# One more split of an inner product in five P7 stages of a soft-routing kernel, with VectorE's queue, the P7 weight sums and the start of P3 rearranged

## The chip, the cores and the metric

One core of a Trainium2 chip runs the kernel. Its time is device microseconds of one execution, and a figure for a kernel is the median of several runs. TensorE multiplies matrices, VectorE and ScalarE read its results out of PSUM (eight banks, each 512 fp32 columns on 128 partitions), GpSimd and SyncE issue DMAs here (ScalarE issues some too).

## The reference

```python
probs = softmax(router_logits)                  # (16, 512, 8)
for e in range(8):
    output += probs[:, :, e:e+1] * matmul(x, expert_weights[e])
# x (16, 512, 512), expert_weights (8, 512, 2048), output (16, 512, 2048), all float32
```

With the batch flattened there are 8192 rows. The sum over the experts is one product: the operand of a row is its x, times the probability of each of the 8 experts, side by side (8 x 512 long), and the weights of the experts stand one under the other.

## The kernel before, in words

**Outer products.** Rows come in 32 blocks of 256; a row pair q is the blocks 2q and 2q+1. The row pair, the two halves of the experts and the two halves of the output's columns (1024 each) make a 2 x 2 by 2 x 2 block product, which is done in seven products P1 to P7 instead of eight (the scheme of Strassen and Winograd) on sums and differences of operands and of weights. In the names of the code r is the number of the outer product (`product(r, q)`, `lefts[r, q]`, `right[r]`).

**Inner products.** Each outer product of a row pair is split in the same manner again. It becomes seven inner products (`STEPS`: 1, 5, 6, 2, 7, 3, 4 in time), each of 8 matrix multiplications of 128 x 128 by 128 x 512. "Step p" is one inner product p, and about 1.73 us of TensorE. Step 6 needs the operand difference `s2` (tile `d`) and accumulates onto the bank of step 1; steps 3 and 7 need the difference `i` (tile `z`), and steps 5, 6, 7 and 4 need weight differences (weight sums, tiles `w`, 128 x 4096), which are made once for each outer product.

**A third split.** In most stages inner products 1 and 5 of the two row pairs are split once more ("by thirds", `by_thirds`): the two row pairs stand as the two rows of a 2 x 2 product, and seven quarter-products take the place of eight. I call them quarters r, again in the order 1, 5, 6, 2, 7, 3, 4; each is 4 multiplications of 128 x 256. Such a split stage has 56 narrow multiplications in place of 32 wide ones. P2's stages of the beginning split inner product 2 (`by_twos`, class `Twos`) as well.

**Stages.** A stage is one or two outer products run together, step by step in turn. By number: 0 to 6 P1; 7 to 14 P2 (14 is called `last2`); 15 (`k5`) two P5; 16 a single P6; 17 to 30 a P6 of one row pair and a P5 of the next; 31 (`k6`) a single P6; 32 (`k7`) to 47 alternate, the even ones P7 and the odd ones P4 of the same two row pairs; 48 (`k3`) a single P3; 49 to 55 two P3 each; 56 a single P3. Inner products 1 and 5 are split in P4's stages from 35 on, and in P3's from 49 to 55. P7's stages are not split: 112 multiplications of 512 columns each.

**The order of the work.** TensorE's, VectorE's and ScalarE's programs are each one list, in the order in which the Python code emits them. For VectorE a planner decides. Work that is not tied to a step (operands, differences, weight sums) is wrapped by `later(cost, make)` into a `Task` and put in a queue. After each step, `slack` moves a clock of TensorE by the step's 1.73 us (0.44 for a quarter) and takes tasks from the queue while VectorE's own clock, which adds up costs, is behind:

```python
def slack(slot=SLOT, lag=LAG):
    clock["dve"] = max(clock["dve"], clock["pe"])
    clock["pe"] += slot
    while queue and clock["dve"] < clock["pe"] - lag:
        queue.popleft().run()
```

Then the step's own reading out of PSUM (the "eviction") is emitted by `post`: VectorE adds a bank to a base in SBUF (`ps<-ps,h`, `h<-ps,h`, `h<-pt,h`), or ScalarE copies it. A task that a step needs and that is not yet done is taken at once (`need`, `flush`). `at(stage, slot, make)` is a hook: `make` runs before step number `slot` of that stage. Hooks fetch weights and bases, put weight sums in the queue, and begin operands of later stages.

**Places of interest.** In stage 14 the hooks at slots 2, 4, 6 and 8 fetch four weight blocks of 1 MB, called `t2` (tile `w` from `wd`, on ScalarE's DMA queue), and slot 9 queues the weight sums 5 and 6 of P6 out of them, each one VectorE operation of 128 x 4096. In stage 14 every step has two evictions in turn, one for each row pair. P7's weight sums 6 and 7 are queued in stages 30 and 31, and 4 in stage 32. P3's weights are loaded into the places of P7's and P4's in stages 46 and 47 (`turnover_in_place(3, ...)`), and its sums 7 and 5 are queued at slot 3 of stage 47, 6 at slot 10, 4 at slot 3 of stage 48. The first P3 is of row pair 5. The first halves of the operands of row pairs 5, 8 and 10 for P3 (`EARLY`) are made during stages 20 and 24, stored, and loaded again in stage 47.

Of the kernel before, what the change touches and what calls it, by code (L numbers as in the profile page):

```python
# [31 lines left out]
def kernel(  # L32
# [41 lines left out]
    def x_tile():  # L74
        return xpool.tile([P, C, HQ], f16, name="xs", tag="x")

# [93 lines left out]
    def inner_sums(b, t7=None):  # L170

        w = {1: b[0, 0], 2: b[1, 0], 3: b[1, 1], 7: t7 or b[0, 1]}

        def step(p, x, y):
            if p not in w:
                w[p] = new_w()
            tt(w[p], x, y, SUB)
        return w, {5: lambda: step(5, b[0, 1], b[0, 0]), 6: lambda: step(6, b[1, 1], w[5]),
                   4: lambda: step(4, b[1, 0], w[6]), 7: lambda: step(7, b[1, 1], b[0, 1])}
# [178 lines left out]
    LAG = 0.3  # L358
# [89 lines left out]
    class Left:  # L448
# [35 lines left out]
        def queue_s2(self):  # L484
            def make():
                self.s2 = spool.tile([P, K8, HP], f16, name="d", tag="d")
                tt(self.s2, self.t[0][:, :, ds(HP, HP)], self.t[0][:, :, ds(0, HP)], SUB)
            self.task["s2"] = later(0.69, make)
# [51 lines left out]
    class HalfLoadedLeft(Left):  # L540


        def __init__(self, xb, pb, kept, source):
            super().__init__(xb, pb, kept=kept)
            self.source = source

        def load(self):
            self.t[0] = new_z()
            sp(self.t[0], self.source)

        def queue_make(self, k):
            if k == 0:
                self.task[0] = None
            else:
                super().queue_make(k)
# [14 lines left out]
    class Thirds:  # L570
# [17 lines left out]
        def queue(self):  # L588
            self.a.queue_make(0)
            self.b.queue_make(0)  # L590
            for p in (5, 6, 3, 7):
# [3 lines left out]
            for left in (self.a, self.b):  # L595
                left.queue_make(1)

        def op(self, p, part):
            need(self.task[7])
            a, b = self.a.t[0], self.b.t[0]  # L600
            z = {1: a[:, 0:C], 2: a[:, C:K8], 4: b[:, C:K8]}.get(p)
            return (self.s[p] if z is None else z)[:, :, ds(part * HP, HP)]

    class Right:
# [9 lines left out]
        def queue_sum(self, sums, p, first=False):  # L614
            def make():
                flush(self.task.get({6: 5, 7: 5, 4: 6}.get(p)))
                sums[p]()
            self.task[p] = later(2.29, make, first)
# [32 lines left out]
    class Product:  # L651
# [7 lines left out]
        def step(self, p):  # L659
            b = "q" if p in (5, 3) else "b" if p == 2 else "x"  # L660
            if p in (1, 5):
                self.banks[b] = (bank if p == 1 else bank2)()
# [100 lines left out]
    def left_of(r, q, fresh=True):  # L763
# [22 lines left out]
        if r == 3 and q in EARLY:  # L786
            pa = PBlock(a, P2)
            return HalfLoadedLeft(xblock(a), pa, ZHalf(q, z_places[q]), operand3[q]), [xblock(a), pa]
# [47 lines left out]
    EARLY = {5: (5, 3), 8: (8, 3), 10: (10, 9)}  # L836
    operand3 = {q: dram.tile([P, K8, HQ], f16, name=f"operand3_{q}") for q in EARLY}
    z_room = []

    def z_place(i):  # L840
        def place():
            if i != 2:
                z_room.append(new_w().rearrange("p k (two t) -> p (k two) t", two=2))
            return z_room[-1][:, ds(i // 2 * K8, K8), :]
        return place
    z_places = {q: z_place(i) for i, q in enumerate((5, 8, 10))}
# [93 lines left out]
    def by_twos(stage):  # L940
# [37 lines left out]
        def full(i, p):  # L978
            some[i].step(p)
            slack()  # L980
            some[i].post(p)
# [10 lines left out]

    def queue_lefts(stage):
        if stage in thirds:
            if not thirds[stage].task:
                thirds[stage].queue()
        elif stage < len(stages):
            for p in stages[stage]:
                queue_left(p.left)

    def run(stage):
# [5 lines left out]
        n = by_thirds(stage) if stage in thirds else 0  # L1007
        if stage in twos:
            n = by_twos(stage)
        for i in range(n // 2, len(some[0].steps)):  # L1010
            for p in some:
                for make in hooks.get((stage, n), ()):
                    make()
                p.step(p.steps[i])
                slack()
# [64 lines left out]
    def queue_halves(q, k):  # L1080
        for i in range(2):
            lefts[7, q + i].queue_make(k)
        if k == 0:
            for i in range(2):
                lefts[7, q + i].queue_s2()
    for n, q in enumerate(ORDER_7[1:], 1):
# [7 lines left out]
        for slot, k in ((5, 0), (11, 1)):  # L1094
            at(stage - 1, slot, lambda q=q, k=k: queue_halves(q, k))
# [208 lines left out]
    def turnover_in_place(r, raw, loads, sums):  # L1304
# [15 lines left out]
        for p, where in sums:  # L1320
            def go(p=p):
# [3 lines left out]
                      ((7, (k3 - 1, 3)), (5, (k3 - 1, 3)), (6, (k3 - 1, 10)), (4, (k3, 3))))  # L1325
# [14 lines left out]
    for stage, slot, q, k in ((k3 - 1, 2, 5, 0), (k3 - 1, 6, 5, 1), (k3 - 1, 7, 8, 0), (k3 - 1, 9, 10, 0),  # L1340
                              (k3 - 1, 10, 8, 1), (k3 - 1, 12, 10, 1)):
        left = lefts[3, q]
        at(stage, slot, left.load if k == 0 else left.kept.begin)
    at(k3, 0, load_z(0))
    early_p = {}

    def early_begin(q):
        early_p[q] = PBlock(2 * q, P2, h_tile([P, 2, HQ], f16))
        sp(early_p[q].t, p_dram[2 * q, ds(P2, 2), :].partition_broadcast(P))

    def early_make(q):
        of = lefts[6, q]
        flush(of.task[0])
        u = new_u()
        times(u, 0, of.xb, early_p[q])
        tt(u, u, of.t[0], SUB)
        sp(operand3[q], u)
    for q, (stage, slot) in EARLY.items():
        at(*slots_after(k5 + stage - 1, slot, 7), lambda q=q: early_begin(q))
        at(k5 + stage, slot, lambda q=q: later(2.45, lambda: early_make(q), True))  # L1360
# [14 lines left out]
    third_at(k3 - 1, 6, third3, 3, 5)  # L1375
# [24 lines left out]
    for p in (1, 5):  # L1400
        at(k7 + 1, 6, lambda p=p: third_sum(p, 7))

# [101 lines left out]
```

## Time and profile before

| | |
|---|---|
| median of 3 runs | 1354.31 us (1354.19 to 1354.35) |
| profiled execution, its own time | 1354.04 us |
| its span in the profile | 1352.3 us |
| TensorE (PE) busy | 1345.7 us, 7062 multiplications |
| weight loads (PEld) | 687.9 us, beside the multiplications |
| VectorE (DVE) busy | 1153.5 us, 1446 instructions |
| ScalarE (ACT) busy | 274.7 us |
| GpSimd (POOL) busy | 404.5 us |
| DMA | 346.12 MB, mean 256 GB/s |

The profile is one execution. Its own time is 1.74 us longer than its span, which lasts from the first to the last instruction that is shown. In its rows L133 is the line of all multiplications (`mm`), L110 that of all VectorE's additions, subtractions and products (`tt`); the tile names tell them apart: `ps` and `pt` are PSUM banks (`bank` and `bank2`), `z`, `u`, `xs` and `d` operands, `w` weights, `h` results and bases. A row of the timeline has start, duration, engine, line, operation with tiles, shape and count, and in brackets the idle time ahead of it with what ended it. A row of the stretches (`A:B`) has the length of the stretch and then, in order, busy time (and instructions) of TensorE, its weight loads, VectorE, ScalarE and GpSimd, then TensorE's clock, the DMA share and GB/s.

### The profile page before, as it was taken

How to read it: one execution, taken by the hardware profiler on the slowest of the kernel's cores; microseconds unless marked ns; L12 is line 12 of the kernel's file. 1: busy time of each engine (PE TensorE's matmuls, PEld its weight loads, DVE VectorE, ACT ScalarE, POOL GpSimd, SP SyncE). 2: the span in 40 equal slices, each digit the busy share in tenths (PEclk: the TensorE clock that was granted, in tenths of full speed). 3: DMA queues.
4: the chain of work that ended last, by engine and by line, in shares of the span. 5: the costliest groups of instructions: out<-in, count | busy, mean ns of one | idle time of the engine just before them, and what ended most of it. 6: DMA issues, size and time to landing. Idle time of an engine off the chain costs nothing.

```text
span 1352.3 us, 19284 instructions
## 1 busy us (share of the span) xinstructions
PE 1345.7 (100%) x7062; PEld 687.9 (51%) x7062; DVE 1153.5 (85%) x1446; ACT 274.7 (20%) x573; POOL 404.5 (30%) x619
## 2 busy tenths in 40 slices
PE   9999999999999999999999999999999999999998
PEld 4566655565544444444444444554555455556564
DVE  7878898888889889798887899888988988988886
ACT  3233423232211111111111100110111011224331
POOL 3223323333223332323312113424333221232342
PEclk9999999999999999999999999999999999999999
DMA  9999979999899999999988897999999989999997
GB/s 187 245 221 237 266 243 237 301 301 269 230 322 302 318 282 297 290 315 264 349 265 270 299 328 158 241 263 207 232 249 225 218 223 333 250 252 234 221 167 127
DMA packets 185391, 346.12 MB, mean 256 GB/s; under 512 B 52176, under 2 KB 81488, under 8 KB 181200
## 3 DMA queue, kind: packets, MB, share of 16 engines
q0 software_dynamic: 84960, 176.72, 57.5%
q1 hardware_dynamic: 97024, 146.02, 35.5%
q10 hardware_dynamic: 3312, 22.15, 4.5%
q8 instruction: 55, 0.90, 0.3%
q14 instruction: 40, 0.33, 0.1%
HBM read 203.59 MB, written 173.74 MB: 279 GB/s over the span
## 4 chain that ended last, share of the span: by engine, by line
PE 83%; issue 10%; POOL 3%; DMA 2%; DVE 1%; POOLq 0%; ACT 0%; DVEq 0%
PE ps L133 65%; PE pt L133 18%; POOL out_dram L124 2%; DMA w<-wd 1%; DMA wd<-w 1%; DVE h L110 1%; DMA out_dram<-h 1%; POOL wd L124 0%; DMA w<-in_x_dram 0%; DVE z L110 0%; POOL w L124 0%; POOL xs L124 0%; DVE w L110 0%; DVE ps L110 0%; POOLq L124 0%
## 5 line engine op out<-in xcount | busy, mean ns | idle before, releaser
L133 PE MATMUL ps<-w,z 128*128 128x512 f16 (+1 forms) x3784 | 818.3, 372 | 0.3 <-DVE z L110 0.3
L133 PEld LDWEIGHTS <-z 128*128 128x128 f16 x5256 | 514.1, 98 | 546.5 <-DVE z L110 0.8
L124 POOL DMA_DIRECT2D out_dram<-h x380 | 249.2, 663 | 729.7 <-ACT h L704 321.8
L133 PE MATMUL pt<-w,z 128*128 128x512 f16 (+1 forms) x1444 | 286.3, 343 | 0.0
L110 DVE TENSOR_TENSOR h<-ps,h 128x512 f32<-128x512 f32 x298 | 202.3, 687 | 81.5 <-PE ps L133 68.2
L110 DVE TENSOR_TENSOR z<-xT,pT 128x2048 f16<-128x2048 f16 x189 | 228.2, 1217 | 0.8 <-DMA xT<-xs 0.8
L133 PE MATMUL ps<-w,d 128*128 128x512 f16 x880 | 199.9, 379 | 0.6 <-DVE ps L110 0.6
L691 ACT COPY h<-ps 128x512 f32<-128x512 f32 x102 | 59.8, 586 | 393.9 <-PE ps L133 382.9
L133 PEld LDWEIGHTS <-d 128*128 128x128 f16 x880 | 86.1, 98 | 98.4 <-issue 1.2
L110 DVE TENSOR_TENSOR z<-z,d 128x2048 f16<-128x2048 f16 x110 | 132.0, 1217 | 0.0
L110 DVE TENSOR_TENSOR w<-w 128x1024 f16<-128x1024 f16 (+2 forms) x102 | 115.2, 1145 | 3.2 <-DMA w<-wd 2.4
L110 DVE TENSOR_TENSOR h<-pt,h 128x512 f32<-128x512 f32 x95 | 64.9, 687 | 32.4 <-PE pt L133 30.3
L704 ACT COPY h<-ps 128x512 f32<-128x512 f32 x54 | 31.6, 586 | 289.8 <-PE ps L133 247.2
L110 DVE TENSOR_TENSOR d<-z 128x1024 f16<-128x1024 f16 x110 | 73.5, 685 | 0.7
L110 DVE TENSOR_TENSOR ps<-ps,h 128x256 f32<-128x256 f32 (+1 forms) x84 | 50.5, 603 | 21.4 <-PE ps L133 16.8
L687 ACT COPY h<-ps 128x512 f32<-128x512 f32 x89 | 49.9, 599 | 69.8 <-PE ps L133 67.0
L124 POOL DMA_DIRECT2D kept<-h x56 | 30.7, 549 | 87.7 <-DVE h L110 47.2
L110 DVE TENSOR_TENSOR z<-z 128x2048 f16<-128x2048 f16 (+1 forms) x52 | 50.5, 978 | 1.6
L683 ACT COPY ps<-ps 128x512 f32<-128x512 f32 x47 | 26.8, 570 | 107.9 <-PE ps L133 71.6
L110 DVE TENSOR_TENSOR h<-h 128x512 f32<-128x512 f32 (+2 forms) x69 | 45.1, 675 | 0.1
L124 POOL DMA_DIRECT2D out_dram<-kept x40 | 41.1, 1134 | 0.3 <-issue 0.2
L133 PEld LDWEIGHTS <-h 128*128 128x128 f16 x384 | 37.5, 98 | 4.4
(99 smaller groups left out, 645.2 us busy)
## 6 DMA issues: line engine op xcount, KB each, us to landing
out_dram<-h POOLq DMA_DIRECT2D x380, 256.0 KB, 7.0
z<-z SPq DMA_DIRECT2D x56, 512.0 KB, 8.1
pT<-p_dram SPq DMA_DIRECT2D x94, 256.0 KB, 7.5
h<-kept SPq DMA_DIRECT2D x88, 256.0 KB, 7.4
w<-wd ACTq DMA_DIRECT2D x20, 1024.0 KB, 9.0
w<-in_expert_weights_dram POOLq DMA_DIRECT2D x33, 512.0 KB, 11.3
xT<-x SPq DMA_DIRECT2D x64, 256.0 KB, 6.5
h<-out_dram SPq DMA_DIRECT2D x60, 256.0 KB, 8.1
```

Of the source, the lines that this page charges most:

```text
L110: dve(nc.vector.tensor_tensor(out=o, in0=a, in1=b, op=op))
L124: note(nc.gpsimd.dma_start(out=o, in_=i, **how))
L133: note(nc.tensor.matmul(ps, z, w, start=start, stop=stop, skip_group_check=True))
L683: act(nc.scalar.copy(self.banks["b"], x))
L687: act(nc.scalar.copy(o[tn], q if p == 5 else x))
L691: act(nc.scalar.copy(o[TN[p]], b if p == 2 else x))
L704: act(nc.scalar.copy(o[tn], b))
```

## The change

Several parts, all in the same program:

- **A third split in P7.** In stages 38, 40, 42, 44 and 46 inner product 1 of the two row pairs is done as seven quarters (class `Ones`, `by_ones`). Inner product 5 stays whole. The order of the first part of such a stage is: quarter 1, quarter 5, step 5 of the first row pair, quarters 6, 2, 3 and 7, step 5 of the second, quarter 4, step 6 of the first, and so on.
- **Copies over used operands.** ScalarE's fp32 copies of quarters 5 and 6 lie in the bytes of the operand sums 5 and 6, which have just been multiplied; no new tile is taken for them.
- **Weight sums for the quarters** (`ones_sum`, four of 128 x 1024), once, in stages 34 and 36.
- **VectorE's queue.** `slack` gets a third limit, `late`. Where it is given, a queued task may be taken as long as it ends, by the planner's clocks, at most `LATE` (2.6 us; `LATE_TWOS` 1.6 in `by_twos`) after the step's end. It holds for steps 4 to 11 of all stages with two products, and in `by_ones` for all whole steps but 5.
- **P7's weight sums in halves:** two operations of 128 x 2048 each instead of one of 128 x 4096 (`in_halves`).
- **Operands of P4's split stages:** the second operand halves are queued ahead of the sums for the quarters (`whole_first`).
- **P3 begins with row pair 11,** both of whose operand halves are made early, in stages 26 and 27 (`EARLY` has pairs of row pair and half now; 10 is out), stored and loaded. The order of the row pairs in P3 changes, and with it the place of those kept. P3's weight sums 7 and 5 are queued at slot 8 of stage 47 (before: 3), 6 at slot 11 (before: 10).

```diff
-    def slack(slot=SLOT, lag=LAG):
+    def slack(slot=SLOT, lag=LAG, late=None):
         clock["dve"] = max(clock["dve"], clock["pe"])
         clock["pe"] += slot
-        while queue and clock["dve"] < clock["pe"] - lag:
+        while queue and clock["dve"] < (clock["pe"] - lag if late is None else clock["pe"] + late - queue[0].cost):
             queue.popleft().run()
...
+    def in_halves(make, first=False):
+        if first:
+            t = later(1.22, lambda: make(1), True)
+            later(1.22, lambda: make(0), True)
+            return t
+        later(1.22, lambda: make(0))
+        return later(1.22, lambda: make(1))
...
-            self.task[p] = later(2.29, make, first)
+            self.task[p] = in_halves(lambda e: make(ds(e * C, C)), first) if halves else later(2.29, make, first)
...
-                right[r].queue_sum(right[r].sums, p, first)
+                right[r].queue_sum(right[r].sums, p, first, r == 7)
...
+    def by_ones(stage):
...
+            slack(0.4375, 1.3)
+            if r == 1:
+                act(nc.scalar.copy(g[:, c0], x[:, c0]))
+            elif r == 5:
+                keep[5] = of.room[5].bitcast(f32)
+                act(nc.scalar.copy(keep[5], q[:, c1]))
+            elif r == 6:
+                keep[6] = of.room[6].bitcast(f32)
+                act(nc.scalar.copy(keep[6], x[:, c0]))
+            elif r == 7:
+                evacuated(0.42)
+                tt(h[:, c1], x[:, c0], keep[5], ADD)
+            elif r == 3:
+                evacuated(0.42)
+                tt(g[:, c1], q[:, c1], keep[6], ADD)
+                some[0].post(1)
+            elif r == 4:
+                act(nc.scalar.copy(h[:, c0], x[:, c0]))
+                some[1].post(1)
...
+            some[i].step(p, (qa, qb)[i])
+            slack(late=LATE if p != 5 else None)
+            some[i].post(p)
+        for slot, todo in enumerate((((1,), (5,)), ((0, 5),), ((6,), (2,), (3,), (7,)), ((1, 5),),
+                                     ((4,), (0, 6)), ((0, 2),), ((1, 6),), ((1, 2),))):
...
-                slack()
+                slack(late=LATE if len(some) == 2 and 4 <= n < 12 else None)
...
-    EARLY = {5: (5, 3), 8: (8, 3), 10: (10, 9)}
+    EARLY = {(5, 0): (5, 3), (8, 0): (8, 3), (11, 0): (11, 3), (11, 1): (12, 3)}
...
-    k3 = add(product(3, 5))
-    for q in ((8, 10), (0, 14), (1, 2), (3, 4), (6, 7), (9, 11), (12, 13)):
+    k3 = add(product(3, 11))
+    for q in ((8, 5), (0, 1), (2, 3), (4, 14), (6, 7), (9, 10), (12, 13)):
...
-                      ((7, (k3 - 1, 3)), (5, (k3 - 1, 3)), (6, (k3 - 1, 10)), (4, (k3, 3))))
+                      ((7, (k3 - 1, 8)), (5, (k3 - 1, 8)), (6, (k3 - 1, 11)), (4, (k3, 3))))
...
-    third_at(k3 - 1, 6, third3, 3, 5)
+    third_at(k3 - 1, 9, third3, 3, 5)
...
+    ONES = k7 + 6
+    for r, where in zip((5, 6, 4, 7), ((ONES - 4, 9), (ONES - 4, 10), (ONES - 2, 9), (ONES - 2, 10))):
+        at(*where, lambda r=r: ones_sum(r))
+    for stage in range(ONES, k3, 2):
+        ones_[stage] = Ones(*(p.left for p in stages[stage]), ones7)
```

More of the change, by code (lines that the diff above doesn't have):

```diff
@@ L357 @@
     HP = HQ // 2
-    LAG = 0.3
+    LAG, LATE, LATE_TWOS = 0.3, 2.6, 1.6
     queue = deque()
@@ L594, in queue @@
                 left.queue_s2()
-            for left in (self.a, self.b):
-                left.queue_make(1)
+            if not whole_first:
+                self.a.queue_make(1)
+                self.b.queue_make(1)
         def op(self, p, part):
@@ L991, in by_twos, with small, full @@
         return 10
+    ones_ = {}
+    def by_ones(stage):
+        some, of = stages[stage], ones_[stage]
+        c0, c1 = (ds(i * HQ, HQ) for i in range(2))
+        x, q = bank2(), bank2()
+        g, qa = bank(), bank()
+        h, qb = bank(), bank()
+        some[0].banks["x"], some[1].banks["x"] = g, h
+        keep = {}
+        def small(r):
+            o = q[:, c1] if r in (5, 3) else g[:, c0] if r == 2 else x[:, c0]
+            z, w = of.op(r), of.weights[r]
+            for c in range(C):
+                mm(o, z[:, c, :], w[:, c, :], r in (1, 5) and c == 0, c == C - 1)
+            slack(0.4375, 1.3)
[17 more added lines that the diff above has]
+                some[1].post(1)
+        def full(i, p):
+            some[i].step(p, (qa, qb)[i])
[3 more added lines that the diff above has]
+                                     ((4,), (0, 6)), ((0, 2),), ((1, 6),), ((1, 2),))):
+            for make in hooks.get((stage, slot), ()):
+                make()
+            if slot == 1:
+                queue_lefts(stage + 1)
+            if slot == 5:
+                store_loads(stage + 1)
+            if slot == 7:
+                finish_loads(stage + 2)
+            for what in todo:
+                (small if len(what) == 1 else full)(*what)
+        return 8
     def queue_lefts(stage):
@@ L995, in queue_lefts @@
             if not thirds[stage].task:
-                thirds[stage].queue()
+                thirds[stage].queue(k7 <= stage < k3)
         elif stage < len(stages):
@@ L1083, in queue_halves @@
         if k == 0:
+            if stage in ones_:
+                ones_[stage].queue()
             for i in range(2):
```

135 lines of the change are left out of this document (92 added, 43 removed).

## The prediction

> **What bounds the kernel now.** The page comes first: its span, its busy times, and the slices of TensorE's clock, which are full throughout. Then the chain of waits, asked for TensorE alone.
>
> ```profile
> span 1352.3 us, 19284 instructions
> PE 1345.7 (100%) x7062; PEld 687.9 (51%) x7062; DVE 1153.5 (85%) x1446; ACT 274.7 (20%) x573; POOL 404.5 (30%) x619
> PEclk9999999999999999999999999999999999999999
> PE ps L133 <- DVE ps L110: 0.6, 2, 0.4
> PE ps L133 <- DVE z L110: 0.3, 1, 0.3
> ```
>
> TensorE streams from end to end, and behind the first microseconds it waits three times, each time for VectorE. So the time is the number of columns that stream plus these waits, and a change can act on it only by fewer columns, or by waits that come or go. The price of a column is read from the timeline, from stretches without a wait (start, duration, engine, operation, count; the duration of the last multiplication of a run overlaps the next, so I take start to start):
>
> ```profile
> 1136.61 1.04 PE L133 MATMUL pt<-w,z 128*128 128x256 f16 x8
> 1137.48 0.60 PE L133 MATMUL ps<-w,u 128*128 128x256 f16 x4
> 1142.72 3.62 PE L133 MATMUL ps<-w,d 128*128 128x512 f16 x16
> 1146.18 5.34 PE L133 MATMUL ps<-w,z 128*128 128x512 f16 x24
> 416.97 1.89 PE L133 MATMUL pt<-w,z 128*128 128x512 f16 x8
> 419.25 1.89 PE L133 MATMUL ps<-w,d 128*128 128x512 f16 x8 [0.39 <-DVE ps L110]
> 420.98 3.62 PE L133 MATMUL ps<-w,z 128*128 128x512 f16 x16
> ```
>
> Eight multiplications of 512 columns take 420.98 - 419.25 = 1.73 us (sixteen take 1146.18 - 1142.72 = 3.46), or 0.216 each; eight of 256 take 0.87 us, and the 56 of a split stage 1142.72 - 1136.61 = 6.11 us, or 0.109 each. The half width costs half: the weight loads stay hidden. The first of the three waits stands here too: 419.25 - 416.97 = 2.28 us for eight, so 0.55 us too much (the waits view shows only 0.39 of it, since a modelled end lies later than the next free start).
>
> **Term 1, the split.** In each of the stages 38, 40, 42, 44 and 46, sixteen multiplications of 512 columns (inner product 1 of two row pairs) become 7 x 4 = 28 of 256: 16 x 0.216 = 3.45 against 28 x 0.109 = 3.05, so 0.40 us less. Five stages: **-2.0 us**. The program built from the change has 60 more multiplications (5 x 12), as this says.
>
> Is that price safe? The Trainium skill (TensorE: Matmul & The Clock Gate, section Back-to-back issue gap) gives for a sustained stream about 81 ns at 128 columns and 131 at 512; on a line between them 256 columns would take some 98 ns (an estimate from that page), 28 of them 2.74 us against 2.10 for the sixteen, and the change would cost 3.2 us in five stages. The rows above disagree with it at both widths (0.216 and 0.109), so the rows decide. Their own break-even is 3.45/28 = 0.123 us for each of the 28.
>
> **What VectorE and ScalarE pay.** The rows by form:
>
> ```profile
> L110 DVE TENSOR_TENSOR z<-z 128x512 f16<-128x512 f16 x16 | 6.4, 422 | 0.3
> L110 DVE TENSOR_TENSOR ps<-pt,z 128x256 f32<-128x256 f32 x24 | 10.4, 433 | 14.6 <-PE pt L133 14.6
> L110 DVE TENSOR_TENSOR w<-w 128x4096 f16<-128x4096 f16 x24 | 54.6, 2284 | 2.5 <-DMA w<-wd 2.4
> L110 DVE TENSOR_TENSOR w<-w 128x2048 f16<-128x2048 f16 x16 | 19.5, 1221 | 0.2
> L110 DVE TENSOR_TENSOR w<-w 128x1024 f16<-128x1024 f16 x62 | 41.1, 685 | 0.4
> L917 ACT COPY h<-ps 128x256 f32<-128x256 f32 x28 | 10.4, 372 | 1.4
> 778.90:803.10 24.20, 24.20 (x114) 10.98 (x112) 22.27 (x24) 1.17 (x2) 4.34 (x8) 1.00 0.85 322
> 969.90:994.10 24.20, 24.20 (x115) 11.01 (x113) 19.70 (x26) 1.17 (x2) 8.03 (x12) 1.00 1.00 213
> 994.10:1017.40 23.30, 23.30 (x138) 13.22 (x136) 20.73 (x27) 4.09 (x10) 8.57 (x11) 1.00 1.04 247
> ```
>
> Each new stage adds four operand sums (4 x 0.42) and two additions out of PSUM (2 x 0.43), 2.55 us of VectorE, and four copies of 0.37 on ScalarE, which is busy for 1.17 of 24.20. A P7 and P4 stage together (second and third window) keep VectorE busy for 40.4 of 47.5 us; afterwards it is 43.0 of 47.1, or 91%. Stage 32 (first window) runs at 22.27/24.20 = 92% without a wait of TensorE, so I put this at nothing; the cover is 4 us per pair. The four weight sums of a quarter (4 x 0.69, once) and the halved sums (two of 1.22 for one of 2.28) lie in that cover too. Of the early operands of P3, one more pair of operations runs in stages 26 and 27, where VectorE has about a tenth free, and the two it replaces leave stage 48; their store and load are one DMA more on SP's queue, tens of microseconds ahead of use.
>
> Inside the new stage the tightest place is quarter 4, which accumulates onto the bank that VectorE must first have read for quarter 7. Between the end of quarter 3 and that start lie quarter 7 and a full step, 0.44 + 1.73 = 2.17 us; VectorE must start (0.27 after the end of a product) and do 0.43 + 0.70 + 0.43, so 1.83 us. 0.3 us are left, if VectorE is free then: the pair of 1.22 us operations that the order puts before it ends, by the same durations, just as quarter 3 ends.
>
> ```profile
> 1139.67 1.04 PE L133 MATMUL pt<-w,xs 128*128 128x256 f16 x8
> 1140.38 0.85 DVE L110 TENSOR_TENSOR ps<-pt,h 128x256 f32<-128x256 f32 x2 [1.47 <-PE pt L133]
> ```
>
> (The 0.27: the first four of these eight end at 1140.11, VectorE starts at 1140.38.) I take 0 for it, between 0 and 0.1 us in each of five stages.
>
> **Term 2, two waits that go.** The order of VectorE's instructions changes in all stages, since the new limits LATE let queued work run ahead of evictions.
>
> ```profile
> 767.20 2.28 DVE L110 TENSOR_TENSOR w<-w 128x4096 f16<-128x4096 f16 x1
> 768.04 1.89 PE L133 MATMUL pt<-w,z 128*128 128x512 f16 x8
> 769.40 0.69 DVE L110 TENSOR_TENSOR ps<-ps,h 128x512 f32<-128x512 f32 x1
> 770.14 1.89 PE L133 MATMUL ps<-w,d 128*128 128x512 f16 x8 [0.22 <-DVE ps L110]
> 1145.43 4.61 DVE L110 TENSOR_TENSOR w<-w 128x4096 f16<-128x4096 f16 x2
> 1150.55 1.22 DVE L110 TENSOR_TENSOR z<-z,d 128x2048 f16<-128x2048 f16 x1
> 1151.83 10.53 PE L133 MATMUL ps<-w,z 128*128 128x512 f16 x48 [0.31 <-DVE z L110]
> ```
>
> In the single stage 31 a whole weight sum (2.28) stands ahead of the eviction that step 6 needs: 770.14 - 768.04 = 2.10, so 0.37 us lost. In the new order one half of the sum stands before the additions of h and the other behind the eviction, which can start when step 1 has ended (768.04 + 0.27) and is done by 769.0; step 6 is due at 769.77. **-0.37 us.** In stage 47 two weight sums stand ahead of the second operand of step 7: 1151.83 - 1146.18 = 5.65 for 24, 0.47 too much. In the new order both operands come before both sums, some 4 us earlier. **-0.47 us.** What is late next there is step 6 of stage 48, whose weights come out of the third sum: behind the two sums, six evictions and a difference it ends, by 2.28 and 0.6 each, about 4 us before its step.
>
> **Term 3, a wait that grows.** The first wait, in the single stage 16, is the end of an unbroken run of VectorE that begins with a DMA:
>
> ```profile
> 386.06 2.29 DVE L110 TENSOR_TENSOR w<-w 128x4096 f16<-128x4096 f16 x1 [1.00 <-DMA w<-wd]
> 388.27 1.28 DVE L110 TENSOR_TENSOR h<-pt,h 128x512 f32<-128x512 f32 x2
> 391.00 2.29 DVE L110 TENSOR_TENSOR w<-w 128x4096 f16<-128x4096 f16 x1 [1.44 <-DMA w<-wd]
> 393.20 1.28 DVE L110 TENSOR_TENSOR h<-ps,h 128x512 f32<-128x512 f32 x2
> 411.79 5.34 PE L133 MATMUL ps<-w,z 128*128 128x512 f16 x24
> 418.51 0.69 DVE L110 TENSOR_TENSOR ps<-ps,h 128x512 f32<-128x512 f32 x1
> w<-wd ACTq DMA_DIRECT2D x20, 1024.0 KB, 9.0
> ```
>
> Today the two evictions h<-pt fill the time in which the second weight sum waits for its load. In the new order that sum stands ahead of them: it still starts at 391.00, and the two come after it, 1.20 us (two starts of 0.60). From there to 418.51 I find no idle time of VectorE, and both orders hold the same operations up to this eviction; so it ends 1.2 us later, at 420.4 instead of 419.2. Step 6 was due at 416.97 + 1.73 = 418.70: 1.8 us lost instead of 0.55 (a part falls in stage 15 already: the last step there, due at 411.79 + 1.73 = 413.52, waits for an eviction that a moved operand difference delays to about 414.5). **+1.25 us**, if the load lands when it does now. One microsecond earlier or later moves it by as much, down to a wait of 0.
>
> **Sum.** -2.0 - 0.37 - 0.47 + 1.25 = -1.6 us. The profiled execution took 1354.04 us (its span and 1.74 around it), so 1352.4; the median of the runs lies 0.27 higher, at 1354.31: **1352.7**. Its own range, with the load landing within a microsecond of today and up to 0.5 us in the new stages, is 1351.7 to 1354.2. A measurement of this kernel can tell about 0.2%, 2.7 us, from no change: 1351.6 and 1357.0 are the borders, so this is no change.
>
> **Rivals.** *All three waits go.* The load of term 3 took some 12 us after its issue; the group's median is 9.0. Were it to land 2 us earlier, the sum would start right behind the eviction before it, and no wait would be left: 1354.31 - 2.0 - 0.37 - 0.47 - 0.55 = 1350.9, faster by just over 0.2%. For it: DMA times shift with every other transfer, and I read the place by hand. Against it: the load's issue and its neighbours on ScalarE's queue stand as before. *The quarters stall.* If VectorE reaches the eviction of quarter 7 late, because the pair of 1.22 us operations at the head of the stage starts late, TensorE waits in each of five stages. A whole pair, 2.4 less 0.3, is 2.1 us each: 1352.7 + 10.5 = 1363. It ends slower than the border from (1357.0 - 1352.7)/5 + 0.3 = 1.2 us of lateness. For it: VectorE runs in order at 91%. Against it: the split stages of today leave VectorE 1.47 us idle at their like place. *The load lands 4 us later,* beyond 395: 1357 or more. *The narrow products are dear,* over 0.123 us each: at the skill's ratio the sum would be 1352.7 + 5.2 = 1358; the rows exclude it nearly.
>
> **How the numbers follow.** The forecast 0.48; all waits gone 0.40 (a hand count of an order is easily off by one operation, and one is enough); stalled quarters 0.08; the later load 0.03; dear products 0.01. So faster 0.40, same 0.48, slower 0.12. The range runs from 1350.7 (the second case less the 0.2 us by which runs and roundings differ) to 1355.2 (the forecast and half a microsecond of the second rival's stall in each of the five stages) and leaves out about 12 in 100.
>
> **What would show it.** In the new profile: 7122 multiplications; P7 stages from 38 on 23.8 us long instead of 24.2; no wait of TensorE in stages 31 and 47; and in the waits view one for "DVE ps" around 417 and one just before it, 1.8 us together by their starts. The forecast is wrong if that wait is absent or if the two additions out of PSUM in the new stages have TensorE wait behind them.

## The result and the profile after

The changed kernel takes 1351.39 us (median of 15 runs; eleven of them lie between 1350.99 and 1351.82) against 1354.39 us for the kernel before in runs beside it. One of the fifteen, at 2390.37 us and a granted clock of 0.556, is left out of the comparison. The ratio of the others is 0.9982, with a 95% interval of 0.9975 to 0.999, so the gain is clear of noise: 3.0 us by the medians, 2.4 by the ratio. The two differ because three runs of the changed kernel lie further up, at 1353.28, 1354.97 and 1355.92 us; of the 15 of the kernel before none lies more than 0.5 us above the median. The gain is right at the border of 0.2% that the prediction set, and the time lies inside the range that was given, 1.3 us under the point. All three waits of the first trace are absent, as in the first rival (1350.9); but one of them is absent from two of three traces of the kernel before as well, as the experiments show.

The page of the changed kernel, and its waits of TensorE:

```profile
span 1349.4 us, 19491 instructions
PE 1343.5 (100%) x7122; PEld 693.1 (51%) x7122; DVE 1166.6 (86%) x1483; ACT 281.8 (21%) x593; POOL 403.9 (30%) x619
PE every L95 <- DVE h L92: 1.3, 1, 1.3
PE ps L136 <- DMA w<-in_x_dram: 0.4, 1, 0.4
PE ps L136 <- DVE lg L304: 0.3, 1, 0.3
PE pt L136 <- DMA w<-in_expert_weights_dram: 0.2, 1, 0.2
```

There are 60 multiplications more, and VectorE works 13 us longer. The three waits for "DVE ps" and "DVE z" of before are gone; what is left belongs to the first 20 us. (The lines have moved by three: L136 is `mm`, L113 is `tt`.)

From start to start of TensorE's multiplications the two traces close. The columns make 1342.36 - 1340.38 = 1.98 us. The waits of stages 16, 31 and 47 made 0.55 + 0.38 + 0.47 = 1.40. What TensorE loses ahead of 25 us (from here on "the start", counted from its first multiplication) went the other way, from 3.15 to 3.68, by 0.53. Together that is 2.85 us; the spans differ by 2.9. (Of the start, 1.9 us are no waits in either trace: the first multiplications, `every<-h`, follow each other at 0.43 us instead of 0.216.)

A split stage and the P4 stage behind it, as stretches:

```profile
968.98:992.76 23.78, 23.78 (x125) 12.10 (x124) 21.27 (x28) 2.63 (x6) 8.15 (x12) 1.00 1.04 237
992.76:1016.14 23.38, 23.38 (x137) 13.31 (x136) 21.39 (x30) 4.09 (x10) 8.52 (x12) 1.00 1.02 232
```

The new stage is 23.78 us long where 24.17 stood, and TensorE is busy for all of it. VectorE works 42.7 of the 47.2 us of the pair. In the place that the prediction called the tightest, the timeline of that stage shows (quarters 3 and 7 are `pt<-w,xs`, then comes a step 5, then quarter 4 as `pt<-d,z`):

```profile
972.46 1.04 PE L136 MATMUL pt<-w,xs 128*128 128x256 f16 x8
973.17 0.43 DVE L113 TENSOR_TENSOR ps<-pt,xs 128x256 f32<-128x256 f32 x1 [0.29 <-PE pt L136]
973.33 1.89 PE L136 MATMUL ps<-w,z 128*128 128x512 f16 x8
973.63 0.70 DVE L113 TENSOR_TENSOR ps<-ps,h 128x512 f32<-128x512 f32 x1
974.24 0.42 DVE L113 TENSOR_TENSOR ps<-pt,xs 128x256 f32<-128x256 f32 x1
975.06 0.60 PE L136 MATMUL pt<-d,z 128*128 128x256 f16 x4
```

VectorE is idle for 0.29 us ahead of the three operations, so it comes in time. They end at 974.66, and quarter 4 begins at 975.06: 0.40 us are left. In the other four new stages VectorE's starts lie at the same distance from TensorE's, to 0.01 us.

### The profile page after: what moved, and what is told of

It is laid out like the page before. It is cut to its first block, busy times and chain, and to the rows that moved or that the text cites. A ratio compares the mean times of both kernels' runs of the same rounds, so it can differ in the third digit from the quotient of the medians.

```text
span 1349.4 us, 19491 instructions
## 1 busy us (share of the span) xinstructions
PE 1343.5 (100%) x7122; PEld 693.1 (51%) x7122; DVE 1166.6 (86%) x1483; ACT 281.8 (21%) x593; POOL 403.9 (30%) x619
## 4 chain that ended last, share of the span: by engine, by line
PE 99%; DMA 1%; POOL 0%; issue 0%; ACT 0%; POOLq 0%
PE ps L136 78%; PE pt L136 21%; DMA w<-in_expert_weights_dram 1%; POOL w L127 0%; ACT h L1568 0%; POOL ident L234 0%; POOLq L234 0%; POOLq L1615 0%
## 5 line engine op out<-in xcount | busy, mean ns | idle before, releaser
L136 PE MATMUL ps<-w,z 128*128 128x512 f16 (+1 forms) x3884 | 840.1, 372 | 0.0
L136 PEld LDWEIGHTS <-z 128*128 128x128 f16 x5236 | 511.7, 98 | 538.1 <-issue 0.3
L113 DVE TENSOR_TENSOR h<-ps,h 128x512 f32<-128x512 f32 x318 | 214.6, 684 | 59.2 <-PE ps L136 58.1
L136 PE MATMUL pt<-w,z 128*128 128x512 f16 (+1 forms) x1304 | 253.2, 338 | 0.2 <-DMA w<-in_expert_weights_dram 0.2
L113 DVE TENSOR_TENSOR z<-xT,pT 128x2048 f16<-128x2048 f16 x188 | 226.5, 1216 | 2.2 <-DMA xT<-xs 2.2
L136 PE MATMUL ps<-w,d 128*128 128x512 f16 x880 | 200.7, 379 | 0.0
L136 PEld LDWEIGHTS <-d 128*128 128x128 f16 x880 | 86.0, 98 | 96.5
L113 DVE TENSOR_TENSOR z<-z,d 128x2048 f16<-128x2048 f16 x110 | 131.7, 1216 | 0.0
L113 DVE TENSOR_TENSOR w<-w 128x1024 f16<-128x1024 f16 (+2 forms) x106 | 116.0, 1113 | 2.6 <-PE ps L136 1.0
L113 DVE TENSOR_TENSOR d<-z 128x1024 f16<-128x1024 f16 x110 | 74.0, 684 | 1.0
L113 DVE TENSOR_TENSOR h<-pt,h 128x512 f32<-128x512 f32 x75 | 51.3, 686 | 27.0 <-PE pt L136 22.8
L113 DVE TENSOR_TENSOR ps<-ps,h 128x256 f32<-128x256 f32 (+1 forms) x84 | 50.6, 603 | 21.0 <-PE ps L136 15.1
L113 DVE TENSOR_TENSOR z<-z 128x2048 f16<-128x2048 f16 (+1 forms) x52 | 50.5, 977 | 1.5
L113 DVE TENSOR_TENSOR h<-h 128x512 f32<-128x512 f32 (+2 forms) x69 | 45.0, 674 | 0.1
L136 PEld LDWEIGHTS <-h 128*128 128x128 f16 x384 | 37.5, 98 | 4.4
```

Source lines behind the costliest of these rows:

```text
L113: dve(nc.vector.tensor_tensor(out=o, in0=a, in1=b, op=op))
L136: note(nc.tensor.matmul(ps, z, w, start=start, stop=stop, skip_group_check=True))
```

## The experiments

**Where the gain comes from.** The first one takes the split out and leaves the rest.

```diff
-    for r, where in zip((5, 6, 4, 7), ((ONES - 4, 9), (ONES - 4, 10), (ONES - 2, 9), (ONES - 2, 10))):
-        at(*where, lambda r=r: ones_sum(r))
-    for stage in range(ONES, k3, 2):
+    for stage in range(k3, k3, 2):
```

> The changed kernel without the third split in P7 (stages 38 to 46 are whole again, and the four weight sums for the quarters are left out); everything else as changed. Theory A (the gain is a sum of columns and waits): the five stages are 24.17 us long again instead of 23.78, 2.0 us in all, and the waits of stages 16, 31 and 47 stay away: 1351.4 + 2.0 = 1353.4 us, 1.0 us under the kernel before. Rival B (most of the gain is VectorE's order, and the split stages only seem shorter because no wait falls into them): 1351.4 to 1352.0. Rival C (VectorE, relieved of 2.55 us per stage, gives nothing back, but the split had cost stalls somewhere else): under 1353.

1353.84 us, 2.45 more than the changed kernel. In its trace the columns are back to 1342.37 us, 1.99 more, and none of the three waits has returned. This execution took 2.77 us more than the traced one of the changed kernel; the rest of it is a single wait of 0.52 us at 140 us, which no other trace here shows (it is for a copy of ScalarE's, and that one stands behind a copy that waited for a DMA, `kept<-h`), and a start that cost 0.2 us more. Theory A holds for the columns: the split alone is worth 2 us. What the other parts are worth without it is too small for these runs: the ratio to the kernel before is 0.9999 (0.999 to 1.0008), and the medians differ by 0.5 us.

The second one switches LATE off.

```diff
-    LAG, LATE, LATE_TWOS = 0.3, 2.6, 1.6
+    LAG, LATE, LATE_TWOS = 0.3, None, None
```

> The changed kernel with the limits LATE and LATE_TWOS switched off, so that queued VectorE work goes by the old limit everywhere; split, halves and the P3 part as changed. Theory A (LATE only removes the wait of stage 16, since 31 goes by the halves and 47 by the P3 sums that are queued later): the wait in stage 16 is back, 0.4 to 0.6 us, 1351.9 us, and the split stages stay 23.8 us long. Rival B (LATE is what keeps VectorE ahead of the quarters): TensorE waits about 1 us in each of five stages for an addition out of PSUM, 1356 us or more. Rival C (the wait of stage 16 hangs on when the load lands, not on the order): no wait, 1351.4.

1352.92 us, 1.5 more. Stage 16 has no wait, as rival C had it. Nearly the whole difference is one wait of 1.26 us at the quarters of stage 47, a place that none of the three theories named:

```profile
1136.86 2.61 DVE L113 TENSOR_TENSOR w<-w 128x1024 f16<-128x1024 f16 x4
1139.39 0.76 DVE L113 TENSOR_TENSOR ps<-pt,h 128x256 f32<-128x256 f32 x2
1139.87 0.60 PE L136 MATMUL pt<-w,z 128*128 128x256 f16 x4 [1.09 <-DVE ps L113]
```

Without LATE the four weight sums for P3's quarters are put right ahead of an addition out of PSUM that TensorE needs; with LATE they start at 1133.3 and are out of the way. The split stages need no LATE: none of them waits.

The third makes P7's weight sums whole again.

```diff
-                right[r].queue_sum(right[r].sums, p, first, r == 7)
+                right[r].queue_sum(right[r].sums, p, first, False)
```

> The changed kernel with P7's weight sums whole again (three operations of 128 x 4096 for six of 128 x 2048). Theory A (the halves are what removes the wait of stage 31): step 6 of stage 31 waits 0.37 us again, 1351.8 us. Rival B (the earlier running of queued work in stage 30 has taken the sum out of the way): no wait there, 1351.4. In both the rest is unchanged, within 0.2 us.

1352.09 us, 0.7 more. Stage 31 waits 0.38 us, to the hundredth what it waited before, behind the same 2.29 us operation:

```profile
767.63 2.29 DVE L113 TENSOR_TENSOR w<-w 128x4096 f16<-128x4096 f16 x1
769.83 0.69 DVE L113 TENSOR_TENSOR ps<-ps,h 128x512 f32<-128x512 f32 x1
770.58 1.89 PE L136 MATMUL ps<-w,d 128*128 128x512 f16 x8 [0.22 <-DVE ps L113]
```

With the halves (the changed kernel) the eviction starts 0.2 us after the step whose bank it reads has ended at 768.01, and step 6 begins after a step 5 of 1.73 us, without a wait:

```profile
768.01 1.89 PE L136 MATMUL pt<-w,z 128*128 128x512 f16 x8
768.22 0.70 DVE L113 TENSOR_TENSOR ps<-ps,h 128x512 f32<-128x512 f32 x1 [0.76 <-PE ps L136]
768.83 1.21 DVE L113 TENSOR_TENSOR w<-w 128x2048 f16<-128x2048 f16 x1
769.74 1.89 PE L136 MATMUL ps<-w,d 128*128 128x512 f16 x8
```

So the halves are what removes it (theory A). The start cost 0.47 us more in this execution (4.15 for 3.68); with the 0.38 that is the 0.85 us by which it took longer than the traced one of the changed kernel.

The fourth and the fifth are on stage 47: P3's sums at the slots of before, and the whole start of P3 as before.

```diff
-                      ((7, (k3 - 1, 8)), (5, (k3 - 1, 8)), (6, (k3 - 1, 11)), (4, (k3, 3))))
+                      ((7, (k3 - 1, 3)), (5, (k3 - 1, 3)), (6, (k3 - 1, 10)), (4, (k3, 3))))
```

> The changed kernel with P3's weight sums queued at the slots of before (7 and 5 at slot 3 of stage 47, 6 at slot 10); row pair 11 first, split and LATE as changed. Theory A (the later slots remove the wait of stage 47): the two sums stand ahead of an operand of step 7 again, 0.3 to 0.6 us, 1351.8 to 1352.0 us. Rival B (LATE has the operands done before, whatever the slots): no wait, 1351.4 us.

1354.96 us, 3.6 more, and a wait of 2.2 us where 0.3 to 0.6 had been expected:

```profile
1142.93 4.61 DVE L113 TENSOR_TENSOR w<-w 128x4096 f16<-128x4096 f16 x2
1148.06 2.35 DVE L113 TENSOR_TENSOR z<-z,d 128x2048 f16<-128x2048 f16 x2
1149.33 6.86 PE L136 MATMUL ps<-w,z 128*128 128x512 f16 x31 [2.03 <-DVE z L113]
```

Here both operands of step 7 stand behind the two sums, where before only the second did. In the changed kernel both are done ahead of them:

```profile
1142.45 1.22 DVE L113 TENSOR_TENSOR z<-z,d 128x2048 f16<-128x2048 f16 x1
1144.18 1.21 DVE L113 TENSOR_TENSOR z<-z,d 128x2048 f16<-128x2048 f16 x1
1145.92 4.60 DVE L113 TENSOR_TENSOR w<-w 128x4096 f16<-128x4096 f16 x2
```

So with row pair 11 first the later slots are needed, and LATE alone does not put the operands ahead of the sums. The later slots with row pair 5 first were not run. The remaining 1.4 us of the median is not in the trace, whose own execution took 1353.23 at a granted clock of 1.0. Six of the eleven runs show a granted clock of 0.997 or 0.998 and took 1354.96 to 1356.52 us; the other five took 1353.23 to 1354.12. The traces of two other experiments (row pair 5 first again, and six stages, below) show a wait longer than this one with 3.41 us at half clock behind it; that would lose 1.7 us (an estimate from those traces). None of the six was traced, so this cause is not shown.

```diff
-    EARLY = {(5, 0): (5, 3), (8, 0): (8, 3), (11, 0): (11, 3), (11, 1): (12, 3)}
+    EARLY = {5: (5, 3), 8: (8, 3), 10: (10, 9)}
...
-    k3 = add(product(3, 11))
+    k3 = add(product(3, 5))
...
-    for stage in range(ONES, k3, 2):
+    for stage in range(ONES, k3 - 2, 2):
```

> The changed kernel with the start of P3 as before (row pair 5 first, its early operands, the slots of P3's weight sums in stage 47), and the third split in stages 38 to 44 only, since the last stage has no room for its tiles then; LATE and halves as changed. Against the changed kernel 0.4 us of columns are lost. Theory A (the wait of stage 47 goes by the later slots of P3's sums): two weight sums stand ahead of the operand of step 7 again, 0.47 us of wait, 1352.3 us in all. Rival B (it goes by LATE): no wait, 1351.8 us. Rival C (LATE puts still more ahead of that step): over 1 us of wait, 1353 us.

(With stage 46 whole, its inner product 1 takes a weight block of which one quarter has been overwritten by the difference for quarter 7.) 1352.98 us, 1.6 more. Stage 47 waits 0.468 us, as before. Theory A gives 1352.3, and the median lies 0.7 above. The execution in the trace took 1359.92 us, with further waits in stages 19 to 21, 5.1 us in all, that go back to loads that landed late, and 3.41 us at half clock behind the longest of them, so its span says nothing here.

**What became of the wait in stage 16.** The weight sums out of t2 and the wait's place, in the changed kernel:

```profile
384.90 2.29 DVE L113 TENSOR_TENSOR w<-w 128x4096 f16<-128x4096 f16 x1 [1.03 <-PE ps L136]
388.35 2.29 DVE L113 TENSOR_TENSOR w<-w 128x4096 f16<-128x4096 f16 x1 [0.56 <-PE pt L136]
390.56 1.28 DVE L113 TENSOR_TENSOR h<-pt,h 128x512 f32<-128x512 f32 x2
417.50 1.89 PE L136 MATMUL pt<-w,z 128*128 128x512 f16 x8
417.70 0.70 DVE L113 TENSOR_TENSOR ps<-ps,h 128x512 f32<-128x512 f32 x1 [0.46 <-PE ps L136]
419.23 1.89 PE L136 MATMUL ps<-w,d 128*128 128x512 f16 x8
```

The order is the one the prediction read out of the program: the second sum stands ahead of the two evictions `h<-pt`. But neither sum waits for its load. The third t2 load was issued at 373.98 and landed at 384.33; in the first trace of before it was issued at 378.92 and landed at 390.90. Two experiments ask whether the order of stage 14 or another part made that:

```diff
-                slack(late=LATE if len(some) == 2 and 4 <= n < 12 else None)
+                slack(late=LATE if len(some) == 2 and 4 <= n < 12 and stage != last2 else None)
```

> The changed kernel with LATE switched off in stage 14 alone, where the two weight sums out of t2 stand. Theory A (the third t2 load is issued 5 us earlier in the changed kernel because it stands elsewhere among the transfers of SyncE and ScalarE in the program, of which eight at a time are under way; the order of VectorE in stage 14 does not matter then): the load still lands near 384, no wait in stage 16, 1351.4 us. Rival B (the order of stage 14 sets both): the load lands near 391 as before and stage 16 waits 0.5 us, 1351.9 us.

1351.67 us, and no wait; the load lands at 385.41. That is what theory A says, but one landing does not decide between the two, as the next runs show.

The other is the kernel before with nothing but the new limits:

```diff
-        while queue and clock["dve"] < clock["pe"] - lag:
+        while queue and clock["dve"] < (clock["pe"] - lag if late is None else clock["pe"] + late - queue[0].cost):
...
-                slack()
+                slack(late=LATE if len(some) == 2 and 4 <= n < 12 else None)
```

> The kernel before with the limits LATE and LATE_TWOS alone (no third split in P7, no halves, P3 and the order of P4's operands as before). Theory A (LATE moves the t2 loads or VectorE so that the wait of stage 16 goes, and does nothing else for the time): 1354.3 - 0.55 = 1353.8 us, and the waits of stages 31 (0.37) and 47 (0.47) stay. Rival B (the prediction's third term: the second weight sum out of t2 stands ahead of two evictions, and the load lands near 391): the wait grows to 1.8 us, 1355.6 us. Rival C (LATE alone does nothing; another part moved the loads): 1354.3.

1354.66 us, ratio 1.0002 (0.9993 to 1.0011). In its trace the load lands at 384.74, stage 16 does not wait, and the waits of stages 31 and 47 stand at 0.38 and 0.47. Rival C: LATE alone is worth nothing in the kernel before. Since even here the wait is absent while the time does not fall, the kernel before itself was run again, twice and unchanged.

> The kernel before once more, for its trace. Theory A (the third t2 load lands near 391 because of the order of transfers in the program): it does so again, within 1 us, and stage 16 waits 0.5 to 0.6 us. Rival B (its landing is a matter of the single execution): it lands anywhere from 385 to 392, and the wait is between 0 and 0.6 us. For TensorE's waits in the first microseconds (3.15 us in the first trace, 3.7 to 4.4 in others) both expect another value between 3.1 and 4.5.

> The same as the run ahead of it, a third trace of the kernel before: theory A the third t2 load near 391 and a wait of 0.5 to 0.6 us in stage 16, rival B another landing and another wait.

The load lands at 388.26 and at 387.99, and stage 16 does not wait in either trace (first of the two):

```profile
389.45 2.28 DVE L110 TENSOR_TENSOR w<-w 128x4096 f16<-128x4096 f16 x1
418.00 1.89 PE L133 MATMUL pt<-w,z 128*128 128x512 f16 x8
418.48 0.69 DVE L110 TENSOR_TENSOR ps<-ps,h 128x512 f32<-128x512 f32 x1
419.73 1.89 PE L133 MATMUL ps<-w,d 128*128 128x512 f16 x8
```

The waits of stages 31 and 47 are there in both, 0.38 and 0.47. So rival B is right: the landing, and the wait of stage 16 with it, is a matter of the single execution. The other traces bear that out. Up to stage 16 the kernel with LATE switched off runs the same instructions in the same order as the kernel before, and seven of the other kernels here the same as the changed one. In the four traces of the old order the load lands at 386.44, 387.99, 388.26 and 390.90, and stage 16 waits only in the last. In the eight of the new order it lands between 384.33 and 387.92, and stage 16 waits in none. So no part of the change is needed for the wait to be absent. Whether the new order makes the load land earlier on the whole stays open, since the two ranges overlap.

The start differs from execution to execution too: 3.15 us in the first trace of before, then 4.17 (of which 0.55 is a wait at 18 us), and 5.40, of which the waits view of the third names

```profile
PE ps L133 <- DMA w<-in_x_dram: 1.6, 1, 1.6
```

and behind that wait TensorE runs at half clock for 3.41 us. With the 0.55 us of stage 16 in the first trace, the losses are 3.70, 4.17 and 5.40 us, and the three executions took 1354.04, 1354.49 and 1355.73 us: the start and that one wait account for their differences to 0.02 us.

The last of this group makes the third and fourth t2 load late.

```diff
-    fetch_at_w(last2, 2 + 2 * i, t2, "t2", kn)
+    fetch_at_w(last2, (2, 4, 9, 9)[i], t2, "t2", kn)
```

> The changed kernel with the third and the fourth t2 load asked for at slot 9 of stage 14 instead of slots 6 and 8, so that they land later; nothing else moved. It puts the prediction's third term to the test. Theory A (the second weight sum out of t2 stands ahead of two evictions, and from it on VectorE is busy without a break up to the eviction that step 6 of stage 16 needs): with the load landing at L (us of the span, 384.3 in the changed kernel) TensorE loses about 1.8 + (L - 391) us around stages 15 and 16, so 1.8 for 391 and 3.8 for 393: 1353 to 1355 us. Rival B (there is idle time of VectorE or slack of TensorE in between that takes up a landing near 391): no wait up to 392, 1351.4 us.

1352.73 us, 1.3 more, in runs that spread from 1351.15 to 1355.94. The load lands at 390.90, as in the first trace of before:

```profile
391.02 2.29 DVE L113 TENSOR_TENSOR w<-w 128x4096 f16<-128x4096 f16 x1 [2.49 <-DMA w<-wd]
418.24 1.89 PE L136 MATMUL pt<-w,z 128*128 128x512 f16 x8
420.04 0.70 DVE L113 TENSOR_TENSOR ps<-ps,h 128x512 f32<-128x512 f32 x1
420.79 1.89 PE L136 MATMUL ps<-w,d 128*128 128x512 f16 x8 [0.66 <-DVE ps L113]
```

The eviction ends at 420.74, where the prediction's run of VectorE had it end at 420.4. TensorE, though, came 1.26 us later than in the first trace of before (418.24 for 416.97), because its start had cost 4.41 us instead of 3.15. So its step was due at 419.97 and waited 0.82 us, not 1.8, and no step of stage 15 waited. Another 0.66 us was lost at 468 us, behind a base that landed late. The mechanism of the third term is thus shown, and its price is set by two times that each move by a microsecond or more between executions: when the load lands, and when TensorE gets there.

**How many stages VectorE has room for.**

```diff
-    ONES = k7 + 6
+    ONES = k7 + 4
...
-    ((ONES - 4, 9), (ONES - 4, 10), (ONES - 2, 9), (ONES - 2, 10))
+    ((ONES - 2, 9), (ONES - 2, 10), (ONES - 1, 7), (ONES - 1, 8))
```

> The changed kernel with the third split in stage 36 too (six stages), its four weight sums made in stages 34 and 35. Theory A (0.39 us for each stage as long as VectorE has room; stages 35 and 36 have 1.5 us of idle VectorE each, and 2.55 are added): 1351.0 us, stage 36 is 23.78 us long. Rival B (VectorE's room does not suffice where the sums of 2.76 us come on top in stages 34 and 35, with 0.3 and 1.5 us idle): a wait of TensorE of 1 us or more there, 1352 or more.

1353.85 us, 2.5 more instead of 0.4 less. The columns do fall by 0.39 us. But in the program's order one more pair of operand operations (2.44 us) is left over at the start of each P7 stage from 38 on and is never caught up with, and where P3 begins VectorE is late:

```profile
1167.50 4.82 DVE L113 TENSOR_TENSOR w<-w 128x1024 f16<-128x1024 f16 x5
1172.23 1.22 DVE L113 TENSOR_TENSOR z<-z,d 128x2048 f16<-128x2048 f16 x1
1173.51 1.90 PE L136 MATMUL ps<-w,z 128*128 128x512 f16 x8 [1.42 <-DVE z L113]
```

Five sums stand ahead of an operand of step 7 in stage 48, and TensorE waits 1.58 us by its starts, and 0.2 us at each of two earlier places. Less the 0.39 us of columns that makes 1.6 us, which is what the fastest of the twelve runs shows (1353.05). Neither theory named this place; rival B had the price. Two of the four sums for the quarters also come a stage earlier here, so what was too much, the split or their place, is not separated. (The execution in the trace took 1360.31 us, since it also lost 5.2 us in stages 20 and 21 to loads that landed late, and ran 3.41 us at half clock behind the second of these waits; four of the twelve runs took 1358.92 us or more.)

```diff
-    ONES = k7 + 6
+    ONES = k7 + 2
...
-    ((ONES - 4, 9), (ONES - 4, 10), (ONES - 2, 9), (ONES - 2, 10))
+    ((ONES - 1, 2), (ONES - 1, 3), (ONES - 1, 8), (ONES - 1, 9))
```

> The changed kernel with the third split in stages 34 and 36 too (seven stages), the four weight sums made in stage 33. Theory A (columns alone decide): 1351.4 - 0.8 = 1350.6 us. Rival B (VectorE becomes the bound for a stretch): in stages 32 to 34 it is busy for 72.0 of 72.1 us already, and 5.3 us are added; what cannot be put off to stages 35 and 36 makes TensorE wait, 2 to 4 us in stages 33 to 35, 1353 to 1355 us.

(The weight difference for quarter 7 is made too late for stage 34 here, which multiplies by the undifferenced block.) 1358.18 us, 6.8 more, ratio 1.0031 (1.0018 to 1.0043). Rival B's place, stages 34 and 35, loses 4.3 us. And there is something in each of the later six split stages:

```profile
PE pt L136 <- DVE ps L113: 3.0, 7, 0.8
882.91 0.68 DVE L113 TENSOR_TENSOR h<-ps,h 128x512 f32<-128x512 f32 x1
883.51 0.42 DVE L113 TENSOR_TENSOR ps<-pt,xs 128x256 f32<-128x256 f32 x1
883.97 0.70 DVE L113 TENSOR_TENSOR ps<-ps,h 128x512 f32<-128x512 f32 x1
884.57 0.42 DVE L113 TENSOR_TENSOR ps<-pt,xs 128x256 f32<-128x256 f32 x1
885.05 0.60 PE L136 MATMUL pt<-d,z 128*128 128x256 f16 x4 [0.37 <-DVE ps L113]
```

The three operations are the same as in the tight place above. An `h` eviction that stands at the wrong side of them holds them up, and quarter 4 waits 0.54 us, six times. This is the prediction's second rival at a quarter of its price, in a kernel with two split stages more. No kernel here beats the changed one.

Not run alone were the order of P4's operands, `LATE_TWOS`, and the start of P3 with row pair 11. Nor is it known which part brings the runs that lie far up. Of the changed kernel and the nine others with LATE, 18 of 109 runs lie over 1.5 us above the median of their kernel; with LATE switched off it is none of 11, and of the kernel before 1 of the 97 beside all these. The two such runs that were traced (1359.92 and 1360.31 us) waited for loads that landed late.

## Why the prediction was right or wrong

**The split (-2.0).** Right: 1.98 us by the columns, 0.39 in each stage, and 2 us when it is taken out. The widths' prices (0.216 and 0.109 us) hold in the new stages, and dear products did not appear. The Trainium skill (TensorE: Matmul & The Clock Gate, section Back-to-back issue gap) also has a formula for a single isolated multiplication, N/2.4 + 2.5 ns. It gives 215.8 and 109.2 ns at these widths, and these sustained streams, at 0.216 and 0.109 us, run at just that and not at the page's sustained 131 ns for 512 columns.

**The cover of VectorE.** Right for the five stages, too generous in words. The prediction put 4 us of room beside each pair of stages. The pair has 4.5 us of idle time by the stretches, but a sixth stage, which asks for 2.55 and has two of the sums for the quarters a stage earlier, costs 2.5 us by the medians and 1.6 in its waits: one pair of operations stays behind in the queue, and where P3 begins its order decides what is late. The tight place was sized well: 0.3 us estimated, 0.40 measured.

**The two waits that go (-0.37, -0.47).** Right, each with its cause: whole weight sums bring back 0.38 in stage 31, the old start of P3 brings back 0.47 in stage 47. The slots are worth more than the sum said, since at the old slots the new order loses 2.2 us there.

**The wait that grows (+1.25).** This is the step that failed. The prediction took one wait of one profiled execution as the kernel's, with the condition "if the load lands when it does now". The load lands between 384 and 391 in the traces of these kernels, and at 388 twice in the kernel before; stage 16 did not wait in either. The argument that the load's issue stood as before was wrong as well: the issue itself lies anywhere between 373.98 and 380.16 in the eight traces of one and the same order. Given a landing at 390.9, the run of VectorE that the prediction added up ended within 0.4 us of its figure. The prediction said what would show it wrong, the absence of this wait, and the wait is absent: the time lies in the range because the range reaches down to the first rival (the forecast's own, 1351.7 to 1354.2, does not hold it), and what set the point apart did not happen.

Without that term the sum is 1354.31 - 2.0 - 0.37 - 0.47 = 1351.5, and 1351.39 was measured. That the two agree to 0.1 us is partly luck, since the start alone differs by more than that between executions. The first rival gave 1350.9 because it also credited the 0.55 us of the wait in stage 16. Two of the three traces of before took 1354.49 and 1355.73 us without that wait, so the median of before, 1354.39, cannot be taken to contain it. The rival's reason, an earlier landing, is what the traces show, but they show it in the kernel before as well.

## What to carry to other kernels

A wait that ends with a DMA in one trace has a price only after a second trace of the same kernel shows it again; the waits between engines alone repeat here to the hundredth of a microsecond (0.38 in stage 31 and 0.47 in stage 47, in five traces each), while the load moves by microseconds. Before costing an order that a load decides, note how far the load's landing is from the point where it matters, and count the term by that chance. And idle time of a nearly full engine is not room: ask which instruction the added work stands ahead of, at the next place where the order is fixed by a deadline.

## What the runs showed of the hardware that was not expected

The same 1 MB load, in the same order of instructions, landed between 384.3 and 387.9 us in eight traces, and between 386.4 and 390.9 in the four of the other order. In the first trace of before, SyncE's and ScalarE's transfers are tied together: from 363.8 to 379 us, each is issued 0.01 to 0.1 us after the eighth one ahead of it has landed (the second t2 load at 377.67, after a landing at 377.57 of a transfer issued at 363.81; the third at 378.92, after one at 378.84). The records of the trace say why. The transfers of these two queues take turns on eight semaphores, and ScalarE waits until 377.59 for the one that the transfer of 363.81 raises, before it gives the same one to the second t2 load. So the limit of eight is one of this program. A slow transfer of SyncE's thus delays loads on ScalarE's queue, which shows nothing of it in its own order.

TensorE's start cost 3.15, 4.17 and 5.40 us in three traces of one kernel, and 3.5 to 4.5 in the others, the 1.9 us of its first multiplications included.

In three traces the profile records half clock for 3.41 us between stretches at full clock, each time behind a wait: in the third trace of before from 8.19 us, behind a loss of 1.8 us at 7.70; in the kernel with row pair 5 first again from 545.21 us, behind 2.36 us at 544.31; with six stages from 544.94 us, behind 3.85 us at 544.06. In the last two, multiplications of 512 columns then follow each other at 0.427 us. Waits of 2.05 us (seven stages) and 2.20 us (the old slots) had no such stretch behind them, so the length of the wait alone does not decide it in these traces.
